# A hybrid decoder layer on one core: softmax of one block ahead of the other's masks, and longer stretches of one product width

## The chip, the cores and the metric

The kernel runs on one core of a Trainium2 chip. The metric is device time in microseconds, from the start to the end of one execution, as the median over several runs; lower is better. The engines are TensorE (PE in the profile; PEld is its weight loading), VectorE (DVE), ScalarE (ACT), GpSimd (POOL) and SyncE (SP, which issues the loads).

## What is computed

One decoder layer for a sequence of 256 positions, width 2048, in float32. Two mixers run side by side on the normalised input: an RG-LRU branch (a short convolution, a gated linear recurrence, times a GELU) and sliding-window attention with sinks (32 query heads, 4 key heads of 64, window 128, blocks of 128). They are merged by sigmoid gates and projected, and an MLP with squared ReLU follows. Cut from the reference:

```python
h = rmsnorm(x, norm_mix_pre)
xr, yr, q, k, v, g_rnn, g_attn = split(h @ w_in)
y_rnn = rg_lru(conv(xr)) * gelu(yr)
y_att = sliding_window_sink_attention(rope(q), rope(k), v, attn_sinks)
mix = sigmoid(g_rnn) * (y_rnn @ w_rnn_proj) + sigmoid(g_attn) * (y_att @ w_attn_proj)
x = x + rmsnorm(mix @ w_out, norm_mix_post)
u = square(relu(rmsnorm(x, norm_mlp_pre) @ w_mlp_up))        # 2048 -> 8192
x = x + rmsnorm(u @ w_mlp_down, norm_mlp_post)               # 8192 -> 2048
```

In attention the scores of 8 heads of a key head are masked, a maximum is taken over keys and sink, and `p / (sum p + exp(sink - m))` multiplies the values.

## The kernel before

**Split products.** Every large float32 product is made from parts: an operand is written as a high part and a low part, and TensorE adds high times high, high times low and low times high. Activations lie as pairs of parts. Weights come from memory in half-chunks of 512 KB (`wraw`, 128 x 1024): SyncE issues the loads, ScalarE casts the high part (`whi`, L94) and VectorE subtracts to get the low part (`wlo`, L95). The class `Stream` keeps this order for the whole kernel: `half()` hands out the next half-chunk, `ahead(j)` makes sure that the parts of six half-chunks (AHEAD = 6) beyond j have been asked for. There are six buffers each for `whi` and `wlo` and four for `wraw`, so a cast waits until TensorE has done with the half-chunk six places before.

**The three shapes of product.** `a_pair` (L243 to L261) makes 2 x 128 output channels for all 256 positions from 2048 inputs, out of four half-chunks, two per group of 128 channels (`f`). The high part of the weights multiplies the high and the low part of the activations at once, 512 columns wide (L253); the low part multiplies the high activations alone, 256 columns wide (L256). Each half-chunk holds eight tiles of 128 x 128, so it gives eight wide and eight narrow products. `a_pair` is called from `conv` and `gelu` (acts `hT`) and from the MLP's up pass (acts `h2T`); the first two pairs of the up pass are made by `up_step` and `up_pair` instead. At the end of a pair ScalarE copies the narrow half (L260) and VectorE adds the rest (L261). The gate and query passes (`b_pass512`, L271, L273, L275) use 512-wide products with three products per weight tile. The down pass (L1061) uses a seven-product scheme, all 512 wide.

**What sets the order.** The program is a Python trace of tiles; a scheduler gives each engine its instruction order by priority and dependence, and pins (`pin`) or `high_priority` fix some places. Side work is written as generators in the list `waiting`: `keys_values`, `attention(g, ...)`, the merge and `residual`. `pump()` advances the first of them by one `yield`, and the main passes call it once for each stage, so a `yield` is the unit of "one stage later" in the program text.

**Attention.** `attention(g)` rotates and transposes the queries, then `scores(tb, j, ...)` multiplies queries and keys of block `tb` into banks (L537), masks them (`s`, L543) and takes maxima (`stat`, L545). Block 0 sees one block of keys and needs one call, block 1 sees two and needs two. `softmax(tb)` combines maxima with the sink (L552 to L554), takes exponentials on ScalarE (L559, one per head), sums and inverts (L561, L562), and scales on VectorE (L564). `turn_probs(tb)` transposes the probabilities on TensorE (`pt`, L581) and copies the banks with ScalarE (L583); the products with the values (`po`, L607) follow.

**1/rms of the first norm.** `first_norm` runs in the first stage of `keys_values`: for each block of positions it writes 1/rms on a diagonal (`spread`, L424) and lets TensorE spread it over all partitions with a matrix of ones (`pr`, L425); ScalarE copies it to `rT` (L426), which `conv` and `gelu` read much later. The keys are rotated (`k`, L486) with sine and cosine tables (L463, `ss`, `cc`), transposed (`pk`, L503) and copied to `kT`.

**The MLP's start.** Products of the first up pairs for the first block of positions (`up_step(0, ...)`, L954, 256 wide) are put between the transposes of the second block's normalised input `h` (`ptr`, L898; `h` comes from VectorE, L892) in portions 26, 6, 6, 6.

Of the kernel before, what the change touches and what calls it, by code (L numbers as in the profile page):

```python
# [22 lines left out]
ALU = mybir.AluOpType  # L23
AX = mybir.AxisListType

P = 128
D = 2048
S = 256
TB = 2
# [137 lines left out]
def layer(tc, x, g_pre, pos_t, pos_row, inv_freq, vecs, sinks, gains, w_kv, w_q, w_xy, w_rg, w_g, w_rp, w_ap, w_out,  # L167
# [75 lines left out]
    def a_pair(acts, out, prio=0):  # L243


        ps = pair("ps")
        for f in range(2):
            both = ps[:, f].rearrange("p a b -> p (a b)")
            for half in range(2):
                hi, lo = ws.half()  # L250
                act = [acts[kt // 4][:, kt % 4] for kt in range(half * 8, half * 8 + 8)]
                for k, a in enumerate(act):
                    mm(both, hi[:, k * P : k * P + P], a.rearrange("p a b -> p (a b)"),  # L253
                       start=half == 0 and k == 0, stop=False)
                for k, a in enumerate(act):
                    mm(ps[:, f, 1, :], lo[:, k * P : k * P + P], a[:, 0, :], start=False,  # L256
                       stop=half == 1 and k == 7)
                pump()
        with tc.high_priority(prio) if prio else ExitStack():
            nc.scalar.copy(out, ps[:, :, 1, :])  # L260
            nc.vector.tensor_tensor(out, ps[:, :, 0, :], out, ALU.add)  # L261
# [145 lines left out]
    ws.ahead(ws.at - 1)  # L407
    r0, r0h = [], []
    rT = pa.tile([P, S], F32, name="rT")

    def first_norm():

        pr = bank(psm, "pr")
        spread = t2("spread")
        for tb in range(TB):
            r = rms(tb, 0)
            half = st[:, 16 + tb : 17 + tb]
            nc.vector.tensor_scalar(half, r, 0.5, None, ALU.mult)
            r0.append(r)
            r0h.append(half)  # L420
            for t in (cc, ss):
                nc.vector.tensor_scalar(t[:, tb], t[:, tb], r, None, ALU.mult)
            dg = spread[:, tb * P : tb * P + P]
            nc.vector.tensor_scalar(dg, ident, r, None, ALU.mult)  # L424
            mm(pr[:, tb * P : tb * P + P], ones, dg, start=True, stop=True)  # L425
        nc.scalar.copy(rT, pr[:, 0:S])  # L426

    pos_i = pa.tile([P, TB], I32, name="pos_i")
# [63 lines left out]
    def keys_values(banks):  # L492
        yield
        first_norm()
        for tb in range(TB):
            nc.scalar.activation(v_sb[:, tb, :], banks[tb][:, 256:512], AF.Copy, scale=r0[tb])
            k2 = t2("k2")
            k4 = k2.rearrange("p (g c d) -> p g c d", g=NKV, c=2)
            rope(banks[tb][:, 0:256], tb, NKV, [k4[:, :, 0, :], k4[:, :, 1, :]])
            yield  # L500
            ps = bank(psm, "pk")
            for g in range(NKV):
                nc.tensor.transpose(ps[:, g * P : g * P + P], k2[:, g * P : g * P + P], ident)  # L503
            nc.scalar.copy(kT[:, :, tb * P : tb * P + P], ps.rearrange("p (g t) -> p g t", g=NKV))
            yield

    yatt = []

    def attention(g, banks):
# [76 lines left out]

        last_group = g == NKV - 1
        scores(0, 0, [bank(psm, "sc") for par in range(2)])
        scores(1, 0, [bank(psb, "sc") for par in range(2)])
        if not last_group:  # L590
            scores(1, 1, two_banks("sc"))
        softmax(0)
        yield
        if last_group:
            scores(1, 1, [bank(psb, "sc") for par in range(2)])
        softmax(1)
        yield
        turn_probs(0)
        yield
# [355 lines left out]
                  start=(tb, kt) == (0, 0), stop=False)  # L955

    todo = [(j, k) for j in (0, 2, 1, 3, 4, 5) for k in range(8)]
    for q, n in enumerate((26, 6, 6, 6)):
        for j, k in todo[:n]:
            pin(up_step(0, j, k))  # L960
        del todo[:n]
# [323 lines left out]
```

## Time and profile before

| what | value |
|---|---|
| median of 3 runs | 1519.63 us (1518.05 to 1521.94) |
| the profiled execution | 1518.56 us |
| its span | 1516.8 us |
| mean granted TensorE clock | 0.997 |
| loads from memory | 288.60 MB read, 194 GB/s over the span |
| load of half a chunk (`wraw`) | 512.0 KB, 4.3 to 5.2 us to landing |

The span is the time between the first and the last instruction that the profile records; the execution's own time is 1.8 us longer, since it includes what lies around. In a row of groups the columns are line, engine, operation, out<-in, shapes, count, then busy time in us and mean ns of one, then the idle time just before such instructions and what ended it. In a waits row the last numbers are the total us, how often, and the longest. In the chain and the timeline the first two numbers are the start in us from the span's start, and the us that the piece takes; xN counts like instructions in a row, and a bracket tells the idle time ahead and who ended it. Matmuls overlap their neighbours, so the distance from start to start is the cost of one.

### The profile page before, as it was taken

The numbers are of one execution on the slowest core, as the hardware profiler recorded it, in microseconds if no ns is written. First come the engines' busy times: TensorE is split into PE (matmuls) and PEld (weight loads), VectorE is DVE, ScalarE is ACT, GpSimd is POOL, SyncE is SP. The second block draws the span as 40 slices with busy tenths as digits, with TensorE's granted clock in tenths as the row PEclk, the third lists the DMA queues.
The fourth block names the chain that finished last, engine by engine and source line by source line (L and its number), as shares of the span: only waits on it lengthen the run. The fifth ranks groups of instructions, "written<-read, shape, count | busy, mean of one in ns | idle before, by whom it ended". The sixth has DMA issues, their size and how long they took to land.

```text
span 1516.8 us, 20055 instructions
## 1 busy us (share of the span) xinstructions
PE 1496.4 (99%) x7600; PEld 1259.9 (83%) x7600; DVE 1103.0 (73%) x1377; ACT 828.7 (55%) x1143; POOL 5.5 (0%) x11
## 2 busy tenths in 40 slices
PE   9999999999999999999999999999999999999997
PEld 7787778788888888888888888888888888888885
DVE  6666677858769967555657866688886666688897
ACT  6554654747566756443355655555454555555453
POOL 0000000000000000000000000000000000000001
PEclk9999999999999999999999999999999999999998
DMA  6645445455646565555764755566667565566564
GB/s 253 219 143 187 142 131 182 150 186 165 218 157 221 168 208 194 192 183 193 270 220 138 271 192 189 183 189 215 218 200 239 198 189 187 181 236 207 208 212 176
DMA packets 82896, 296.20 MB, mean 195 GB/s; under 512 B 9712, under 2 KB 9968, under 8 KB 81648
## 3 DMA queue, kind: packets, MB, share of 16 engines
q1 hardware_dynamic: 79056, 284.43, 57.3%
q10 hardware_dynamic: 3744, 10.50, 1.9%
q8 instruction: 59, 0.97, 0.3%
q14 instruction: 37, 0.30, 0.1%
HBM read 288.60 MB, written 6.29 MB: 194 GB/s over the span
## 4 chain that ended last, share of the span: by engine, by line
PE 82%; DVE 9%; DMA 5%; ACT 2%; issue 2%; DVEq 0%; SPq 0%; ACTq 0%
PE ps L253 22%; PE ps L256 11%; PE dQ L1061 4%; DMA wraw<-in_w_dn 4%; PE pp L271 4%; PE pp L275 4%; PE pp L273 4%; PE g L271 3%; PE g L275 3%; PE g L273 3%; DVE wlo L95 3%; PE s L1061 2%; PE dP L1061 2%; PE q L273 2%; PE q L275 2%; PE q L271 2%
## 5 line engine op out<-in xcount | busy, mean ns | idle before, releaser
L95 DVE TENSOR_TENSOR wlo<-wraw,whi 128x1024 fp32r<-128x1024 f32 x523 | 635.1, 1223 | 314.0 <-ACT whi L94 313.1
L94 ACT CAST whi<-wraw 128x1024 fp32r<-128x1024 f32 x523 | 544.5, 1052 | 576.6 <-PE ps L253 134.2
L253 PE MATMUL ps<-h2T,whi 128*128 128x512 f32 x960 | 240.5, 393 | 0.0
L253 PEld LDWEIGHTS ps<-h2T,whi 128*128 128x128 f32 x960 | 172.8, 189 | 30.8
L256 PEld LDWEIGHTS ps<-h2T,wlo 128*128 128x128 f32 x960 | 131.0, 191 | 9.3
L256 PE MATMUL ps<-h2T,wlo 128*128 128x256 f32 x960 | 133.9, 283 | 0.0
L253 PE MATMUL ps<-hT,whi 128*128 128x512 f32 x512 | 129.7, 394 | 0.0
L1061 PE MATMUL dQ<-whi,uT 128*128 128x512 f32 x288 | 106.9, 389 | 0.0
L253 PEld LDWEIGHTS ps<-hT,whi 128*128 128x128 f32 x512 | 91.9, 189 | 17.6 <-issue 1.5
L271 PE MATMUL g<-whi,hT 128*128 128x512 f32 x256 | 101.3, 396 | 0.0
L273 PE MATMUL g<-wlo,hT 128*128 128x512 f32 x256 | 100.1, 391 | 0.1
L275 PE MATMUL g<-whi,hT 128*128 128x512 f32 x256 | 99.9, 390 | 0.0
L256 PEld LDWEIGHTS ps<-hT,wlo 128*128 128x128 f32 x512 | 69.9, 190 | 5.0
L256 PE MATMUL ps<-hT,wlo 128*128 128x256 f32 x512 | 71.6, 283 | 0.0
L1061 PEld LDWEIGHTS dQ<-whi,uT 128*128 128x128 f32 x288 | 54.1, 188 | 11.2
L271 PEld LDWEIGHTS g<-whi,hT 128*128 128x128 f32 x256 | 48.1, 188 | 10.5 <-issue 1.0
L1061 PE MATMUL dQ<-wlo,uT 128*128 128x512 f32 x144 | 56.2, 390 | 0.5 <-DVE wlo L95 0.5
L275 PEld LDWEIGHTS g<-whi,hT 128*128 128x128 f32 x256 | 48.1, 188 | 10.1
L273 PEld LDWEIGHTS g<-wlo,hT 128*128 128x128 f32 x256 | 48.2, 188 | 10.0 <-DVE wlo L95 0.5
L1061 PE MATMUL dCs<-whi,uT 128*128 128x512 f32 x144 | 54.1, 389 | 0.0
L1061 PE MATMUL dP<-whi,uT 128*128 128x512 f32 x144 | 54.1, 389 | 0.0
L130 DVE TENSOR_TENSOR tlo<-t,thi 128x1536 fp32r<-128x1536 f32 x28 | 49.2, 1757 | 5.4 <-ACT thi L129 5.3
(280 smaller groups left out, 2464.8 us busy)
## 6 DMA issues: line engine op xcount, KB each, us to landing
wraw<-in_w_up SPq DMA_DIRECT2D x128, 512.0 KB, 4.8
wraw<-in_w_dn SPq DMA_DIRECT2D x128, 512.0 KB, 4.6
wraw<-in_w_g SPq DMA_DIRECT2D x64, 512.0 KB, 4.5
wraw<-in_w_xy SPq DMA_DIRECT2D x64, 512.0 KB, 4.6
wraw<-in_w_q SPq DMA_DIRECT2D x32, 512.0 KB, 4.5
wraw<-in_w_ap SPq DMA_DIRECT2D x32, 512.0 KB, 4.4
wraw<-in_w_rp SPq DMA_DIRECT2D x32, 512.0 KB, 4.3
wraw<-in_w_out SPq DMA_DIRECT2D x32, 512.0 KB, 5.2
```

The lines of the kernel that those rows point to most:

```text
L94: self.pin(self.nc.scalar.copy(hi, src))
L95: self.pin(self.nc.vector.tensor_tensor(lo, src, hi.bitcast(F32), ALU.subtract))
L130: v.tensor_tensor(lo, t, hi.bitcast(F32), ALU.subtract)
L253: mm(both, hi[:, k * P : k * P + P], a.rearrange("p a b -> p (a b)"), start=half == 0 and k == 0, stop=False)
L256: mm(ps[:, f, 1, :], lo[:, k * P : k * P + P], a[:, 0, :], start=False, stop=half == 1 and k == 7)
L271: mm(banks[tb][n], a[:, 0, t], hi[:, n * 512 : n * 512 + 512], start=first, stop=False)
L273: mm(banks[tb][n], a[:, 0, t], lo[:, n * 512 : n * 512 + 512], start=False, stop=False)
L275: mm(banks[tb][n], a[:, 1, t], hi[:, n * 512 : n * 512 + 512], start=False, stop=last)
L1061: mm(b, a[x], w[y], start=not begun and i == 0, stop=tail and i == 2)
```

## The change

Four places change.

`a_pair` keeps its products but makes them in another order: with the half-chunks 0 to 3 of the pair, the high parts of 0 and 1 and the first product of 2 (17 wide products), then the low parts of 0, 1, 2 and 3 (32 narrow ones), then the rest of 2 and all of 3 (15 wide ones). The weights are asked for by `ws.ahead` a little later than before, at the places that the diff shows; `pump` is called four times as before.

In `attention`, `softmax(0)` is called before the scores of block 1 are masked, and two stages are added before `turn_probs(0)`.

The products that spread 1/rms leave `first_norm` for a function `spread_out`, called after the transposes of the first block's keys.

The first portion of `up_step` grows from 26 to 30 products.

```diff
--- before.py
+++ after.py
@@ -244,18 +244,41 @@
 
 
         ps = pair("ps")
-        for f in range(2):
-            both = ps[:, f].rearrange("p a b -> p (a b)")
-            for half in range(2):
-                hi, lo = ws.half()
-                act = [acts[kt // 4][:, kt % 4] for kt in range(half * 8, half * 8 + 8)]
-                for k, a in enumerate(act):
-                    mm(both, hi[:, k * P : k * P + P], a.rearrange("p a b -> p (a b)"),
-                       start=half == 0 and k == 0, stop=False)
-                for k, a in enumerate(act):
-                    mm(ps[:, f, 1, :], lo[:, k * P : k * P + P], a[:, 0, :], start=False,
-                       stop=half == 1 and k == 7)
-                pump()
+
+        def run(j, part, ks=range(8)):
+            f, half = j // 2, j % 2
+            for k in ks:
+                kt = half * 8 + k
+                a, w = acts[kt // 4][:, kt % 4], parts[j][part][:, k * P : k * P + P]
+                if part:
+                    mm(ps[:, f, 1, :], w, a[:, 0, :], start=False, stop=j == 1 and k == 7)
+                else:
+                    mm(ps[:, f].rearrange("p a b -> p (a b)"), w, a.rearrange("p a b -> p (a b)"), start=kt == 0,
+                       stop=j == 3 and k == 7)
+
+
+
+        at = ws.at
+        parts = [ws.half()]
+        run(0, 0)
+        parts.append(ws.half(False))
+        run(1, 0)
+        pump()
+        parts.append(ws.half(False))
+        run(2, 0, (0,))
+        run(0, 1)
+        ws.ahead(at + 1)
+        pump()
+        run(1, 1)
+        ws.ahead(at + 2)
+        run(2, 1)
+        parts.append(ws.half(False))
+        run(3, 1)
+        pump()
+        run(2, 0, range(1, 8))
+        ws.ahead(at + 3)
+        run(3, 0)
+        pump()
         with tc.high_priority(prio) if prio else ExitStack():
             nc.scalar.copy(out, ps[:, :, 1, :])
             nc.vector.tensor_tensor(out, ps[:, :, 0, :], out, ALU.add)
@@ -407,11 +430,10 @@
     ws.ahead(ws.at - 1)
     r0, r0h = [], []
     rT = pa.tile([P, S], F32, name="rT")
+    spread = t2("spread")
 
     def first_norm():
 
-        pr = bank(psm, "pr")
-        spread = t2("spread")
         for tb in range(TB):
             r = rms(tb, 0)
             half = st[:, 16 + tb : 17 + tb]
@@ -420,9 +442,12 @@
             r0h.append(half)
             for t in (cc, ss):
                 nc.vector.tensor_scalar(t[:, tb], t[:, tb], r, None, ALU.mult)
-            dg = spread[:, tb * P : tb * P + P]
-            nc.vector.tensor_scalar(dg, ident, r, None, ALU.mult)
-            mm(pr[:, tb * P : tb * P + P], ones, dg, start=True, stop=True)
+            nc.vector.tensor_scalar(spread[:, tb * P : tb * P + P], ident, r, None, ALU.mult)
+
+    def spread_out():
+        pr = bank(psm, "pr")
+        for tb in range(TB):
+            mm(pr[:, tb * P : tb * P + P], ones, spread[:, tb * P : tb * P + P], start=True, stop=True)
         nc.scalar.copy(rT, pr[:, 0:S])
 
     pos_i = pa.tile([P, TB], I32, name="pos_i")
@@ -502,6 +527,8 @@
             for g in range(NKV):
                 nc.tensor.transpose(ps[:, g * P : g * P + P], k2[:, g * P : g * P + P], ident)
             nc.scalar.copy(kT[:, :, tb * P : tb * P + P], ps.rearrange("p (g t) -> p g t", g=NKV))
+            if tb == 0:
+                spread_out()
             yield
 
     yatt = []
@@ -586,14 +613,16 @@
 
         last_group = g == NKV - 1
         scores(0, 0, [bank(psm, "sc") for par in range(2)])
+        softmax(0)
         scores(1, 0, [bank(psb, "sc") for par in range(2)])
         if not last_group:
             scores(1, 1, two_banks("sc"))
-        softmax(0)
         yield
         if last_group:
             scores(1, 1, [bank(psb, "sc") for par in range(2)])
         softmax(1)
+        yield
+        yield
         yield
         turn_probs(0)
         yield
@@ -955,7 +984,7 @@
                   start=(tb, kt) == (0, 0), stop=False)
 
     todo = [(j, k) for j in (0, 2, 1, 3, 4, 5) for k in range(8)]
-    for q, n in enumerate((26, 6, 6, 6)):
+    for q, n in enumerate((30, 6, 6, 6)):
         for j, k in todo[:n]:
             pin(up_step(0, j, k))
         del todo[:n]
```

How the order of instructions moves is shown at three places. Line numbers grow by 23 to 29 with the change: L543 becomes L570, L552 L579, L561 L588, L581 L608, L425 L450, L503 L528; in `a_pair` wide products are L256 and narrow ones L254 after it.

VectorE, attention of group 1, from the second pair of masks on; before (`mask_422` and `mask_423` are the same mask of both kernels):

```order
L543 SCALAR_TENSOR_TENSOR s<-sc,mask_422 128x512 x2
L545 TENSOR_REDUCE stat<-s 128x2 x2
L543 SCALAR_TENSOR_TENSOR s<-sc,mask_422 128x512 x2
L545 TENSOR_REDUCE stat<-s 128x2 x2
L552 TENSOR_TENSOR stat<-stat,sink 128x8
L95 TENSOR_TENSOR wlo_1437<-wraw_1277,whi_1436 128x1024
L553 TENSOR_SCALAR stat<-stat 128x8
L552 TENSOR_TENSOR stat<-stat,sink 128x8
L554 TENSOR_TENSOR stat<-sink,stat 128x8
L553 TENSOR_SCALAR stat<-stat 128x8
L554 TENSOR_TENSOR stat<-sink,stat 128x8
L95 TENSOR_TENSOR wlo_1467<-wraw_1308,whi_1466 128x1024
```

and with the change:

```order
L570 SCALAR_TENSOR_TENSOR s<-sc,mask_423 128x512
L579 TENSOR_TENSOR stat<-stat,sink 128x8
L570 SCALAR_TENSOR_TENSOR s<-sc,mask_423 128x512
L580 TENSOR_SCALAR stat<-stat 128x8
L572 TENSOR_REDUCE stat<-s 128x2
L581 TENSOR_TENSOR stat<-sink,stat 128x8
L572 TENSOR_REDUCE stat<-s 128x2
L570 SCALAR_TENSOR_TENSOR s<-sc,mask_423 128x512 x2
L572 TENSOR_REDUCE stat<-s 128x2 x2
L588 TENSOR_TENSOR stat<-stat 128x8
L579 TENSOR_TENSOR stat<-stat,sink 128x8
L589 RECIPROCAL stat<-stat 128x8
```

Block 0's statistics (the first L552, L553, L554) stood behind all masks and a low part of weights; now they stand among the first masks of block 1, and the low parts come after them.

TensorE, one `a_pair` of the up pass, its first two half-chunks before:

```order
L253 MATMUL ps<-h2T_6249,whi_8257 128x512 x4
L253 MATMUL ps<-h2T_6250,whi_8257 128x512 x4
L256 MATMUL ps<-h2T_6249,wlo_8258 128x256 x4
L256 MATMUL ps<-h2T_6250,wlo_8258 128x256 x4
L253 MATMUL ps<-h2T_6251,whi_8279 128x512 x4
L253 MATMUL ps<-h2T_6252,whi_8279 128x512 x4
L256 MATMUL ps<-h2T_6251,wlo_8280 128x256 x4
L256 MATMUL ps<-h2T_6252,wlo_8280 128x256 x4
```

and a stretch of one with the change, from the last wide product before the narrow ones:

```order
L256 MATMUL ps<-h2T_6249,whi_8369 128x512
L254 MATMUL ps<-h2T_6249,wlo_8310 128x256 x4
L254 MATMUL ps<-h2T_6250,wlo_8310 128x256 x4
L254 MATMUL ps<-h2T_6251,wlo_8339 128x256 x4
L254 MATMUL ps<-h2T_6252,wlo_8339 128x256 x4
L254 MATMUL ps<-h2T_6249,wlo_8370 128x256 x4
L254 MATMUL ps<-h2T_6250,wlo_8370 128x256 x4
L254 MATMUL ps<-h2T_6251,wlo_8384 128x256 x4
L254 MATMUL ps<-h2T_6252,wlo_8384 128x256 x4
L256 MATMUL ps<-h2T_6249,whi_8369 128x512 x3
```

Eight and eight alternate before; with the change the low parts of four half-chunks follow one another.

TensorE, first gate pass (`g`), where 1/rms is spread; before:

```order
L275 MATMUL g<-whi_399,hT_134 128x512
L425 MATMUL pr<-spread,ones 128x128
L271 MATMUL g<-whi_399,hT_134 128x512
L425 MATMUL pr<-spread,ones 128x128
L273 MATMUL g<-wlo_400,hT_134 128x512
L275 MATMUL g<-whi_399,hT_134 128x512
```

and with the change, some 38 gate products later, behind the first transposes of the keys:

```order
L296 MATMUL g<-wlo_480,hT_136 128x512
L298 MATMUL g<-whi_479,hT_136 128x512
L528 MATMUL pk<-ident,k_512 128x128 x4
L450 MATMUL pr<-spread,ones 128x128 x2
L294 MATMUL g<-whi_479,hT_136 128x512
L296 MATMUL g<-wlo_480,hT_136 128x512
```

The two products of `pr` stood one gate product apart ahead of the keys' transposes; now both stand behind them.

## The prediction

> **What bounds the kernel now.** I read the page first, then TensorE's waits, then the chain that ended last, then the timeline around each edit.
>
> ```profile
> span 1516.8 us, 20055 instructions
> PE 1496.4 (99%) x7600; PEld 1259.9 (83%) x7600; DVE 1103.0 (73%) x1377; ACT 828.7 (55%) x1143; POOL 5.5 (0%) x11
> PEclk9999999999999999999999999999999999999998
> L95 DVE TENSOR_TENSOR wlo<-wraw,whi 128x1024 fp32r<-128x1024 f32 x523 | 635.1, 1223 | 314.0 <-ACT whi L94 313.1
> L253 PE MATMUL ps<-h2T,whi 128*128 128x512 f32 x960 | 240.5, 393 | 0.0
> L253 PE MATMUL ps<-hT,whi 128*128 128x512 f32 x512 | 129.7, 394 | 0.0
> ```
>
> TensorE is busy for 99% of the span at a clock that never leaves the top digit. VectorE is at 73%, ScalarE at 55%, and the products of `a_pair` waited for nothing (0.0). So time can come only from two places: TensorE's stalls, and what its products cost in the stream. The waits view lists the stalls that were recorded:
>
> ```profile
> PE pt L581 <- DVE s L564: 3.6, 3, 1.4
> PE pr L425 <- DVE spread L424: 0.9, 1, 0.9
> PE ptr L898 <- DVE h L892: 0.7, 1, 0.7
> PE s L1061 <- DVE u L261: 0.6, 2, 0.3
> ```
>
> All the rows that the change aims at come to 5.8 us. For the price of a product I take the chain of waits, where start to start is the true spacing (the 393 ns of a row above is latency, with neighbours overlapping):
>
> ```profile
> 827.54 5.76 PE ps L998 x48
> 833.30 1.84 PE ps L995 x8
> ...
> 965.04 1.84 PE ps L253 x8
> ...
> 984.59 1.85 PE ps L253 x8
> ...
> 1067.77 2.72 PE dQ L1061 x12
> ```
>
> In a long stretch of one width a 512-wide product costs 2.72/12 = 226.7 ns and a 256-wide one 5.76/48 = 120.0 ns. Eight and eight would then take 1.813 + 0.960 = 2.773 us. In `a_pair`, from 965.04 to 984.59, seven periods of eight and eight take 19.55/7 = 2.793 us. **One alternation of width costs 20 ns** beyond its products. The eight wide ones behind the 48 narrow ones took 1.84 us, the same as behind eight narrow ones: a longer stretch does not make its edge dearer.
>
> **Part 1, longer stretches.** The same 64 products per pair now run as 32 wide, 32 narrow, since the 15 wide at a pair's end join the 17 at the start of the next: one alternation where there were four. The two counts above, (960 + 512)/32, give 46 pairs. 46 x 3 x 20 ns = 2.76; I take **2.7 us** (2.5 to 2.8; at the ends of the runs of pairs a part alternation stays). No instruction is added. What holds this up is that the low parts of four half-chunks must be there when the 32 narrow products start; see the third rival.
>
> The Trainium skill, "TensorE: Matmul & The Clock Gate", section "Back-to-back issue gap", gives the spacing of a warm product by its width alone, N/2.4 + 2.5 ns. By that the order of widths is worth nothing and this term would be 0. The trace disagrees on the size (216 and 109 ns by the rule, 226.7 and 120.0 measured) and shows the 20 ns that the rule has no room for.
>
> **Part 2, attention.** Groups 1, 2 and 3 stall at the first transposes of the probabilities. Group 1 and group 3:
>
> ```profile
> 160.91 0.39 PE L271 MATMUL q<-whi,hT 128*128 128x512 f32 x1
> 162.73 1.23 PE L581 MATMUL pt<-ident,s 128*128 128x128 f32 x8 [1.43 <-DVE s L564]
> ...
> 269.80 0.39 PE L253 MATMUL ps<-hT,whi 128*128 128x512 f32 x1
> 270.98 1.23 PE L581 MATMUL pt<-ident,s 128*128 128x128 f32 x8 [0.79 <-DVE s L564]
> 280.96 0.63 PE L581 MATMUL pt<-ident,s 128*128 128x128 f32 x4
> ```
>
> By starts, the product at 160.91 would be done after 0.23, at 161.14, so the loss is 1.59; in group 3 it is 0.95; group 2 shows the same 1.43 recorded. Together 4.1 us. Behind it stands softmax on VectorE and ScalarE:
>
> ```profile
> 149.36 1.28 DVE L543 SCALAR_TENSOR_TENSOR s<-sc,mask 128x512 f32<-128x512 f32 x2
> 150.56 1.27 DVE L545 TENSOR_REDUCE stat<-s 128x4 f32<-128x512 f32 x2
> ...
> 156.51 0.16 DVE L552 TENSOR_TENSOR stat<-stat,sink 128x8 f32<-128x8 f32 x1
> ...
> 161.89 1.29 DVE L564 TENSOR_TENSOR s<-s,stat 128x512 f32<-128x512 f32 x2
> ```
>
> ```profile
> 152.95 1.06 ACT L94 CAST whi<-wraw 128x1024 fp32r<-128x1024 f32 x1 [4.76 <-PE g L275]
> ...
> 158.24 0.39 ACT L559 ACTIVATE s<-s,stat 128x128 f32<-128x128 f32 x1
> ...
> 161.42 0.49 ACT L559 ACTIVATE s<-s,stat 128x256 f32<-128x256 f32 x1
> ...
> 279.06 0.49 ACT L559 ACTIVATE s<-s,stat 128x256 f32<-128x256 f32 x1
> ```
>
> Before, all masks and maxima (149.36 to 156.51) and a weight's low part come ahead of block 0's exponentials at 158.24. Now block 0's statistics stand behind its own four passes and, as the order shows, two masks and two maxima of block 1: 149.36 + 2.4 + four more passes of 0.6 gives about 154.1. The eight exponentials, 0.39 apart (158.24 to 161.42), end near 157.2, and sum, reciprocal and the scaling of 1.29 end near 159, or 159.6 with block 1's last masks between. TensorE arrives at about 160.6. The wait goes with about 1 us to spare.
>
> The change says "two stages later", but the order shows the first transposes directly behind the 48 gate products: one q product earlier than before in groups 1 and 2, seven in group 0, so 0.2 and 1.6 us earlier. In group 0, where the waits view names none, I count about 2 us to spare after that. The second block's transposes do move 48 products back in groups 0 to 2. What is late next: ScalarE's copies of the transposed banks and two low parts now stand behind the softmax. The cast at 152.95 had waited 4.76 us for TensorE to free a buffer, so six half-chunks stood ready, each good for 12 products of 0.227, 2.72 us; a slip of 5 us is covered, and uncovered costs up to 1.2 us per low part. I allow 0.1 for each of three groups at a bank copy. In group 3 block 1's exponentials cannot move up, since ScalarE ends them at 279.06 + 0.49 = 279.55 behind the same casts and copies, while TensorE is 0.8 earlier; the transposes at 280.96, with no wait before, then lose about 0.5 (0 to 0.9). Net 4.1 - 0.3 - 0.5 = **3.3 us** (1.8 to 4.4).
>
> **Part 3, 1/rms spread.**
>
> ```profile
> 45.10 0.49 PE L425 MATMUL pr<-spread,ones 128*128 128x128 f32 x2 [0.92 <-DVE spread L424]
> ...
> 49.04 1.28 ACT L463 ACT_TABLE_LOAD   x1
> ...
> 54.22 0.29 DVE L486 TENSOR_TENSOR k<-ra,rb 128x128 f32<-128x128 f32 x1
> 54.57 0.66 PE L503 MATMUL pk<-ident,k 128*128 128x128 f32 x4
> ```
>
> The 0.92 at 45.10 goes. But the keys' transposes at 54.57 come directly behind keys that VectorE ends at 54.22 + 0.29 = 54.51. Their chain runs from the table load at 49.04 through the sines and the rotation, not through TensorE. It comes forward only by the copy of the spread (about 0.4) that leaves ScalarE ahead of the load. TensorE would be there 1.6 us sooner (0.92, some 0.2 of start-up, and 0.5 for the two products now behind). So most of the wait reappears at the keys. Net **0.4 us** (-0.2 to 1.1).
>
> **Parts 4 and 5, MLP edges.**
>
> ```profile
> 812.90 3.27 PE L954 MATMUL ps<-h2T,whi 128*128 128x256 f32 x26
> 816.91 0.66 PE L898 MATMUL ptr<-ident,h 128*128 128x128 f32 x4 [0.74 <-DVE h L892]
> ...
> 999.48 0.50 PE L1061 MATMUL s<-thi,seven 128*128 128x512 f32 x1 [0.29 <-DVE u L261]
> ```
>
> Thirty instead of 26 products fill the 0.74 ahead of the second block's transposes with 4 x 0.12 = **0.5 us** (0.3 to 0.7) of work taken from after them. At the start of each of the two down passes, TensorE waits for the last pair's `u`; in the new order ScalarE's copy of that pair stands one weight cast (1.05 us) earlier, against 0.6 recorded in both. I take **0.4 us** (0 to 0.9).
>
> **Sum**: 2.7 + 3.3 + 0.4 + 0.5 + 0.4 = 7.3 us. The profiled execution took 1518.56 us, its span 1516.8; so 1509.5 for the span and 1511.3 for the execution. The median of the runs shown, 1519.63 (1518.05 to 1521.94), lies 1.1 above that execution, which gives **1512.3 us**. With the terms between their bounds together: 1509.6 to 1515.
>
> **Rivals.**
>
> First, the 20 ns are not the width's: they belong to the handover from one half-chunk to the next, which stays. For it: each period of eight and eight has exactly one handover. Against it: the 12 products in 2.72 at 1067.77 are one half-chunk each and pay no such edge, nor do the 48 narrow ones, which run over several. Then 7.3 - 2.7 = 4.6, **1515.0 us**. The formula of the Trainium skill cited above leads to the same.
>
> Second, the attention's gain is handed on. With both blocks' exponentials in one row on ScalarE, the casts behind them are late and TensorE waits for weights in the gate and q passes instead. For it: VectorE's low parts move behind the softmax and its page row shows 313 us spent waiting for casts. Against it: the six half-chunks ahead. Then 7.3 - 3.3 = 4.0, **1515.6 us**.
>
> Third, slower. The 32 narrow products use four low parts, one per 8 x 0.12 = 0.96 us, while VectorE makes one per 1.22 (1223 ns in its row). If the low parts are not made in advance, each stretch is short by at least 0.26, 46 x 0.26 = 12.0 us, and 12.0 - 7.3 = +4.7 gives **1524.3 us**; with all four made in the burst it would be up to three times that. Parts used in one stretch also free their buffers in one go, which favours bursts. It decides once the split's lead falls from six parts to under four, about 4 us late. Against it:
>
> ```profile
> 913.84 1.05 ACT L94 CAST whi<-wraw 128x1024 fp32r<-128x1024 f32 x1 [1.74 <-PE ps L253]
> ```
>
> In the midst of the MLP pairs ScalarE's cast waits for TensorE to give back a buffer, so the split is full and not behind; four low parts, 4.9 us, fit twice into a pair of 11.2 us, and by the buffers that come free a part is started some 10 us before its use.
>
> **How the numbers follow.** Forecast 0.72, first rival 0.08, second 0.11, third 0.09. About 0.3%, 4.6 us (to 1515.1), is what a measurement of this kernel can tell from no change. The first rival lies on that bound, half to each side; the second falls to no change; of the forecast's own cases a few hundredths fall short of it. So faster 0.74, same 0.16, slower 0.10. The forecast's own range is 1509.6 to 1515; to leave out no more than 2 in 10 I reach to 1508.9 below (all bounds kind) and, past the second rival, to 1517.0 above. The third is left out.
>
> **What would show it.** A period of 32 and 32 in `a_pair` takes 7.25 + 3.84 + 0.02 = 11.11 us instead of 4 x 2.793 = 11.17. In TensorE's waits the row of `pt` for `s` falls from 3.6 to under 0.8, `pr` for `spread` vanishes and a wait of 0.5 to 1.0 for `k` appears, `ptr` for `h` falls to about 0.3. The forecast is wrong if `a_pair`'s narrow products wait for `wlo`, if rows of `g` or `q` waiting for `whi` or `wlo` pass 1 us together, or if the period stays at 11.17.

## The result, and the profile after

| kernel | median | ratio to before, 95% interval |
|---|---|---|
| before, 20 runs | 1518.15 us | |
| changed, 20 runs | 1516.3 us (1512.98 to 1519.6) | 0.9987 (0.998 to 0.9994) |

Ratios are of fast executions; one execution of the experiment sixteens, at a mean clock of 0.654, took 2132.6 us and is not in its ratio. The change gains 0.13%, some 2 us; 7.3 were forecast. The profiled execution's span is 1515.4 us against 1516.8. The first lines of the changed kernel's page, and TensorE's waits:

```profile
span 1515.4 us, 20015 instructions
PE 1493.5 (99%) x7600; PEld 1261.9 (83%) x7600; DVE 1101.4 (73%) x1377; ACT 830.5 (55%) x1143; POOL 5.5 (0%) x11
PEclk9999999999999999999999999999999999999999
```

```profile
PE pt L608 <- ACT pT L610: 4.6, 3, 2.3
PE pt L608 <- DVE s L591: 1.6, 1, 1.6
PE ptr L375 <- DMA x<-in_x: 1.2, 1, 1.2
PE warm L366 <- DVE ones L350: 1.1, 1, 1.1
PE pk L528 <- DVE k L511: 0.8, 1, 0.8
PE dQ L1090 <- DVE wlo L95: 0.8, 1, 0.8
PE kv L396 <- DVE wlo L111: 0.4, 1, 0.4
PE ptr L927 <- DVE h L921: 0.3, 1, 0.3
```

The waits of `pt` for `s` fell from 3.6 to 1.6 us (under 0.8 was forecast), and a row is new: `pt` waits 4.6 us for `pT`, the copies of the transposed banks on ScalarE. To see what each edit brought, the span is cut at TensorE instructions that all kernels of this study share. The numbers are differences between starts in the profiled executions, in us:

| stretch on TensorE | before | changed | changed, again | pairs_only | no_attention | keys_later |
|---|---|---|---|---|---|---|
| start to first gate product (`g`) | 34.79 | 34.72 | 35.60 | 34.63 | 34.65 | 35.89 |
| to first scores (`sc`) | 58.52 | 58.30 | 58.34 | 58.42 | 61.18 | 57.24 |
| to first gate product of the recurrence (`pg`) | 252.08 | 254.66 | 253.07 | 252.01 | 251.97 | 251.97 |
| to the merge's transposes | 271.40 | 270.68 | 270.73 | 270.80 | 270.80 | 270.80 |
| to the last transpose of `h` | 204.25 | 204.22 | 204.25 | 204.25 | 204.25 | 204.25 |
| to the down pass (the first `dQ` from `thi`) | 177.32 | 176.00 | 176.01 | 176.49 | 176.01 | 176.00 |
| to the end | 518.42 | 516.81 | 516.40 | 516.87 | 514.96 | 517.04 |

The third row is attention, and it is the one that got longer: by 2.6 us in one execution of the changed kernel and 1.0 in another. All other stretches together got shorter by 4.0 in the first (1.4 + 2.6). In the first row, 35.60 and 35.89 go with a slow clock and not with an edit: the granted clock was 0.50 from 9.04 to 12.46 us in the one and from 9.38 to 12.79 in the other, and 1.00 there in the rest.

**What happens in attention.** ScalarE, then TensorE, in group 0 of the changed kernel (timeline; a bracket is idle time ahead and who ended it):

```profile
107.01 0.50 ACT L586 ACTIVATE s<-s,stat 128x256 f32<-128x256 f32 x1
...
107.50 2.93 ACT L94 CAST whi<-wraw 128x1024 fp32r<-128x1024 f32 x3
110.33 1.06 ACT L610 COPY s<-pt 128x512 f32<-128x512 f32 x2
...
115.73 1.05 ACT L94 CAST whi<-wraw 128x1024 fp32r<-128x1024 f32 x1 [2.24 <-DMA wraw<-in_w_q]
118.55 1.05 ACT L94 CAST whi<-wraw 128x1024 fp32r<-128x1024 f32 x1 [1.77 <-DMA wraw<-in_w_q]
119.83 1.05 ACT L94 CAST whi<-wraw 128x1024 fp32r<-128x1024 f32 x1 [0.24 <-DMA wraw<-in_w_g]
121.10 1.04 ACT L94 CAST whi<-wraw 128x1024 fp32r<-128x1024 f32 x1 [0.23 <-DMA wraw<-in_w_g]
122.06 1.06 ACT L610 COPY pT<-pt 128x512 f32<-128x512 f32 x2
```

```profile
118.68 1.03 PE L608 MATMUL pt<-ident,s 128*128 128x128 f32 x8
122.69 0.66 PE L608 MATMUL pt<-ident,s 128*128 128x128 f32 x4 [2.27 <-ACT pT L610]
```

Block 1's first eight transposes fill both banks of the pool by 119.7. The casts from 115.73 to 121.10 stand ahead of the copies in ScalarE's order, and each of them first waits for its weights to land (2.24, 1.77, 0.24 and 0.23 us). The copies do not overtake them: ScalarE stands idle for the last 0.23 us while both banks are full. The copies start at 122.06, and TensorE, which needs a bank for the next four transposes, stands still for 2.27 us. In the kernel before, the same copies came at 114.86, ahead of those casts:

```profile
111.64 1.04 ACT L583 COPY s<-pt 128x512 f32<-128x512 f32 x2
...
114.86 1.08 ACT L583 COPY pT<-pt 128x512 f32<-128x512 f32 x2
```

Why are the weights late? The row of DMA activity from 95 to 130 us in 40 slices (tenths of the engines' time; 0.875 us each), before and then changed:

```profile
DMA  4368200000039886100000002685778878476566
```

```profile
DMA  3377100000000000000049879997973898678400
```

Before, loads run in three bursts; changed, one long pause lies from 101 to 112.5 us. A `wraw` buffer is free once VectorE has subtracted the low part. SyncE's waits from 90 to 125 us show it (the last number is the longest wait), before and then changed:

```profile
SPq L76 <- DVE wlo L95: 23.1, 8, 9.6
```

```profile
SPq L76 <- DVE wlo L95: 30.1, 10, 15.9
```

Low parts that stood ahead of the scaling of block 0's probabilities now stand behind that of both blocks, and until they are made there is no buffer to load into. VectorE before (the second of two low parts there), then changed:

```profile
104.56 1.22 DVE L95 TENSOR_TENSOR wlo<-wraw,whi 128x1024 fp32r<-128x1024 f32 x1
```

```profile
108.06 2.50 DVE L591 TENSOR_TENSOR s<-s,stat 128x512 f32<-128x512 f32 x4
110.48 4.62 DVE L95 TENSOR_TENSOR wlo<-wraw,whi 128x1024 fp32r<-128x1024 f32 x4
```

A low part also needs its cast. ScalarE's casts stand behind the exponentials of both blocks now: before, one starts at 101.94 us, ahead of them; changed, none starts between 93.12 and 107.50. So both engines share in the pause.

```profile
101.94 1.05 ACT L94 CAST whi<-wraw 128x1024 fp32r<-128x1024 f32 x1 [1.66 <-PE g L275]
```

**The stall costs more than its length.** Windows of the changed kernel: length, busy us and count of PE, PEld, DVE, ACT, POOL, then the granted clock, the DMA share, GB/s:

```profile
122.50:127.00 4.50, 4.31 (x16) 3.65 (x17) 0.91 (x1) 1.79 (x4) 0.00 (x0) 0.62 0.82 258
124.00:126.70 2.70, 2.70 (x9) 2.22 (x8) 0.00 (x0) 0.59 (x1) 0.00 (x0) 0.50 0.79 232
```

After 2.27 us of standing still TensorE runs at half clock until 126.7, which loses about 4.5 x (1 - 0.62) = 1.7 us more. In the page's row of 40 slices this does not show.

**The pairs** look as forecast. The chain of the changed kernel, in the up pass:

```profile
966.53 3.83 PE ps L254 x32
970.36 7.28 PE ps L256 x32
977.64 3.83 PE ps L254 x32
```

64 products take 977.64 - 966.53 = 11.11 us, 0.06 less than 4 x 2.793.

### The profile page after: what moved, and what is told of

The parts are those of the page before. It is cut to its first block, busy times and chain, and to the rows that moved or that the text cites. A ratio compares the mean times of both kernels' runs of the same rounds, so it can differ in the third digit from the quotient of the medians.

```text
span 1515.4 us, 20015 instructions
## 1 busy us (share of the span) xinstructions
PE 1493.5 (99%) x7600; PEld 1261.9 (83%) x7600; DVE 1101.4 (73%) x1377; ACT 830.5 (55%) x1143; POOL 5.5 (0%) x11
## 4 chain that ended last, share of the span: by engine, by line
PE 77%; DVE 11%; DMA 6%; ACT 3%; issue 2%; DVEq 0%; SPq 0%; ACTq 0%
PE ps L256 21%; PE ps L254 11%; PE dQ L1090 4%; DMA wraw<-in_w_dn 4%; PE pp L296 4%; PE pp L298 4%; PE pp L294 4%; DVE wlo L95 4%; PE g L298 3%; PE g L294 3%; PE g L296 3%; PE s L1090 3%; PE dP L1090 2%; PE o L298 2%; PE o L296 2%
## 5 line engine op out<-in xcount | busy, mean ns | idle before, releaser
L256 PE MATMUL ps<-h2T,whi 128*128 128x512 f32 x960 | 223.9, 390 | 0.0
L256 PEld LDWEIGHTS ps<-h2T,whi 128*128 128x128 f32 x960 | 178.2, 188 | 35.6
L256 PE MATMUL ps<-hT,whi 128*128 128x512 f32 x512 | 121.2, 391 | 0.0
L254 PEld LDWEIGHTS ps<-h2T,wlo 128*128 128x128 f32 x960 | 119.1, 192 | 2.3
L254 PE MATMUL ps<-h2T,wlo 128*128 128x256 f32 x960 | 119.9, 283 | 0.0
L256 PEld LDWEIGHTS ps<-hT,whi 128*128 128x128 f32 x512 | 94.7, 188 | 20.1 <-issue 1.5
L254 PEld LDWEIGHTS ps<-hT,wlo 128*128 128x128 f32 x512 | 63.7, 192 | 1.2
L254 PE MATMUL ps<-hT,wlo 128*128 128x256 f32 x512 | 64.7, 283 | 0.0
```

The source lines that it names most:

```text
L254: mm(ps[:, f, 1, :], w, a[:, 0, :], start=False, stop=j == 1 and k == 7)
L256: mm(ps[:, f].rearrange("p a b -> p (a b)"), w, a.rearrange("p a b -> p (a b)"), start=kt == 0, stop=j == 3 and k == 7)
```

## The experiments

Each ratio is to the kernel before, on the same chip. "Stretch" is attention's, from the first scores to the first `pg`, in the profiled execution.

**1. pairs_only**: the kernel before with `a_pair` of the changed one.

```diff
-            for half in range(2):
-                hi, lo = ws.half()
...
+        run(0, 0)
...
+        run(1, 0)
...
+        run(2, 0, (0,))
+        run(0, 1)
...
+        run(1, 1)
...
+        run(2, 1)
...
+        run(3, 1)
...
+        run(2, 0, range(1, 8))
...
+        run(3, 0)
```

> The kernel before with the new order of products in a_pair alone. Theory: the long stretches are worth what the changed kernel's trace suggests, about 3.3 us in a_pair, and the last pair's copy ahead of the down passes another 1 us: some 4 us below the kernel before (ratio 0.9972), a period of 64 products near 11.1 us, narrow products that wait for no low part. Rival: the price belongs to the handover of half-chunks and the gain in the changed kernel came from elsewhere: ratio 1.000, period 11.17 us. Second rival: the low parts are short in the stretch of 32: slower, with waits of narrow products for wlo.

Measured: 0.9975 (0.9966 to 0.9984), 1515.09 us, a pair of 11.12 us, no wait of a narrow product for `wlo`. By the medians this part alone is worth more than the whole change; the intervals just overlap. The two waits at the start of the down passes (0.6 us in the row of waits, 0.9 by starts) are gone too.

**2. sixteens**: the kernel before with stretches of 16.

```diff
-            for half in range(2):
-                hi, lo = ws.half()
+            two = [ws.half() for half in range(2)]
+            for part in range(2):
+                for half in range(2):
+                    for k in range(8):
+                        kt = half * 8 + k
+                        a, w = acts[kt // 4][:, kt % 4], two[half][part][:, k * P : k * P + P]
...
```

> The kernel before with a_pair in stretches of 16 wide and 16 narrow products: two alternations of width per pair instead of four, while the handovers of half-chunks stay as they are. Theory (each alternation has a price): two thirds of what one alternation per pair saves, 46 x 2 x 20 to 24 ns = 1.8 to 2.2 us in a_pair, a pair of 11.13 us, ratio 0.9985. Rival (the handover has the price, or the longest stretch alone): 11.17 us a pair, ratio 1.000.

Measured: 0.9975 (0.9965 to 0.9986). The chain of this kernel:

```profile
961.00 3.65 PE ps L258 x16
964.66 1.91 PE ps L256 x16
966.57 3.65 PE ps L258 x16
970.23 1.91 PE ps L256 x16
972.14 3.65 PE ps L258 x16
```

64 products take 11.14 us, where four alternations take 11.17 and one takes 11.11: the price goes with the number of alternations, some 20 ns each, and the handovers, which stayed, have none. By the ratio this kernel gained more than its alternations, 46 x 0.03 = 1.4 us, as pairs_only did, and here too the waits at the start of the down passes are gone. The traces show why: ahead of the first down pass ScalarE's copy of the last pair starts 0.95 us after the pair's products, here and in pairs_only, and 1.9 us after them in the kernel before, where a weight cast stands between.

**3. no_attention**: the changed kernel with attention as before.

```diff
-        softmax(0)
         scores(1, 0, [bank(psb, "sc") for par in range(2)])
...
+        softmax(0)
         yield
...
         softmax(1)
         yield
-        yield
-        yield
         turn_probs(0)
```

> The changed kernel with attention as before. Theory: the attention edit costs about 3.5 to 4 us net, so this is 5 us below the kernel before (ratio 0.9967), with the waits of pt for s of the kernel before (3.6 us) and none of pt for pT. Rival: the attention edit gained what was forecast and another edit gave it back: then this is slower than the changed kernel, ratio about 1.001.

Measured: 0.9975 (0.9962 to 0.9987), 1514.61 us; waits of `pt` for `s` 4.4, none for `pT`; stretch 251.97. So by the stretch the attention edit costs 2.7 us in the first profile of the changed kernel and 1.1 in the second; the intervals of the times overlap. The profiled execution shows another stall, at the keys, and with it why the gain can fall short of 0.9967:

```profile
55.07 0.66 PE L528 MATMUL pk<-ident,k 128*128 128x128 f32 x4 [2.19 <-DVE k L511]
...
56.00:59.00 3.00, 3.00 (x10) 2.39 (x9) 1.62 (x5) 0.97 (x3) 0.00 (x0) 0.54 0.68 231
```

In this execution a load landed late (a cast waited 1.30 us for it), the keys came 1.3 us later, the wait was 2.19 us, and the clock halved for 3 us again (0.54 in the window behind it).

**4. early_no_yields and yields_only**: the two halves of the attention edit, each alone, with all other edits of the changed kernel.

```diff
         softmax(1)
         yield
-        yield
-        yield
         turn_probs(0)
```

> The changed kernel without the two added stages; softmax(0) stays ahead of block 1's masks. In the order the first transposes then stand behind 26 to 31 of the 48 gate products. Theory: the stages hold these transposes back, and without them TensorE reaches them 6 to 7 us after the scores while s is ready some 9 us after them: waits of pt for s of 2 to 3 us in each of groups 0 to 2, ratio 1.000 to 1.002; the waits for pT vanish. Rival: the stages alone are what costs and the early softmax is all gain: waits at pt below 2 us in all, ratio 0.994 to 0.996.

```diff
-        softmax(0)
         scores(1, 0, [bank(psb, "sc") for par in range(2)])
...
+        softmax(0)
         yield
```

> The changed kernel with the two added stages, but softmax(0) behind block 1's masks as before. Theory: the copies of block 1's banks stand behind weight casts that wait for loads because the transposes come 48 products later, so pt waits for pT 4 to 5 us in groups 0 to 2 here too, and the first transposes wait 1.4 us for s in groups 1 and 2: 4 to 5 us above no_attention, ratio 0.999 to 1.000. Rival: it is the early softmax that starves the loads: then no wait for pT, and the time is that of no_attention, ratio 0.9967.

Measured: early_no_yields 1.0002 (0.9992 to 1.0012), stretch 255.92, `pt` waits for `s` 6.9 us in 4 places, the longest 1.9, none for `pT`. yields_only 0.9997 (0.9988 to 1.0006), stretch 255.64, `pt` waits for `s` 4.5 and for `pT` 3.2. Both theories held in kind; the waits were 1.4 to 1.9 rather than 2 to 3 us, and 3.2 rather than 4 to 5. Each half alone costs about what the pairs gain. With the early softmax alone the scheduler puts the first transposes 17 to 22 products ahead of their place in the changed kernel, before the data is there; the stages hold them back, but carry block 1's copies behind the casts. In groups 1 and 2 yields_only waits 1.31 and 1.67 us for a bank, the changed kernel 0.99 and 1.35, so there the stages alone make the wait. In group 0 yields_only waits only 0.35 us for a bank where the changed kernel waits 2.4, and its loads pause as in the kernel before: the long pause belongs to the early softmax.

**5. second_none**: the two stages between the transposes of block 0 and block 1 taken out.

```diff
         turn_probs(0)
-        yield
-        yield
         turn_probs(1)
```

> The changed kernel without the two stages between the transposes of block 0 and those of block 1; everything else stays. Block 1's transposes then come 3 to 6 products behind block 0's instead of 48, and ScalarE's copies of their banks stand ahead of the weight casts that wait for loads. Theory (the place of the copies in ScalarE's queue is what cost): the 4 to 5 us of pt for pT go, and with them the slow stretch of TensorE in group 0; pt waits for s some 1 to 1.5 us in groups 1 and 2 since block 1's softmax is just ending: about 3 to 4 us below the changed kernel, ratio 0.9955 to 0.9970. Rival (the early softmax itself keeps the copies late): waits for pT of 3 us or more stay, ratio 0.998 to 0.999.

Measured: 1.0001 (0.9991 to 1.001), stretch 255.71: the forecast was wrong by 0.3 to 0.5%. The waits for `pT` went, as the theory said:

```profile
PE pt L608 <- DVE s L591: 5.3, 3, 1.8
PE pt L608 <- ACT s L610: 1.6, 1, 1.6
```

But the softmax of block 1 ends later than assumed, so that `pt` waits 5.3 us for `s`, and in group 0 1.6 us for block 0's own copies, which stand behind three casts. Behind the wait in group 1, 1.84 us, the clock halved for 3.4 us, which is 1.7 us more. Neither 3 nor 48 products behind is right.

**6. mid24 and mid12**: the distance between the two, 24 and 12 products; both with the keys' transposes later (experiment 7).

```diff
         turn_probs(0)
         yield
-        yield
         turn_probs(1)
```

and in mid12 also

```diff
-        waiting.append(attention(g, b_pass512(hT, [bank(psb, f"q{tb}") for tb in range(TB)])))
+        waiting.append(attention(g, b_pass512(hT, [bank(psb, f"q{tb}") for tb in range(TB)], 1)))
```

> The changed kernel with the keys' transposes 6 products later (as in keys_later) and one stage instead of two between the transposes of block 0 and block 1, which then stand 24 products apart instead of 48. ScalarE has two or three weight casts ahead of the copies instead of four or five, and the last of them waits for a load. Theory: waits for pT remain, some 1 to 1.5 us in each of groups 0 to 2, less than in the changed kernel; the stretch from the first scores to the first gate product of the recurrence takes 251 to 253.5 us (254.7 in the changed kernel, 252.0 with attention as before); ratio 0.9965 to 0.998. Rival (the loads are late because of the early softmax, wherever the copies stand): as the changed kernel, 254 us or more.

> As mid24, and the query pass calls for side work after each half-chunk, so that the transposes of block 1 stand 12 products behind those of block 0: late enough for its softmax, and with the copies ahead of the casts that wait for loads. Theory: pt waits for neither s nor pT in groups 0 to 2 (under 1.5 us together); only group 3 keeps 1.8 us for s; the stretch takes 248 to 250 us, and the kernel is 2 to 4 us below keys_later, ratio 0.9945 to 0.9957, the fastest of all. Rival (the gain of the early softmax is always handed on): the waits come back elsewhere in the stretch, which stays at 252 us or more.

Measured: mid24 1.0007 (0.9998 to 1.0017), stretch 256.59, waits for `pT` 6.4 us, up to 2.3, and a window at clock 0.66 behind one of them. mid12 0.9976 (0.9967 to 0.9986), stretch 253.25, waits for `pT` 4.2, up to 1.6. Both forecasts were too good, and both rivals named the stretch rightly (254 us or more, 252 us or more). ScalarE in mid24 and then in mid12, group 1:

```profile
167.45 2.00 ACT L94 CAST whi<-wraw 128x1024 fp32r<-128x1024 f32 x2
171.75 1.04 ACT L94 CAST whi<-wraw 128x1024 fp32r<-128x1024 f32 x1 [2.31 <-DMA wraw<-in_w_q]
172.70 1.06 ACT L613 COPY pT<-pt 128x512 f32<-128x512 f32 x2
```

```profile
166.43 1.99 ACT L94 CAST whi<-wraw 128x1024 fp32r<-128x1024 f32 x2
168.31 1.07 ACT L613 COPY pT<-pt 128x512 f32<-128x512 f32 x2
```

In mid24 the last cast ahead waits 2.31 us for a load. In mid12 no load is waited for, and the two casts themselves, 1.99 us, still make TensorE wait 1.59 us (`pt` at 168.96). Both place the copies behind casts, and that is the cost; the loads decide how large it is.

**7. keys_later**: no_attention with four more stages ahead of the first keys' transposes, which move by 6 products.

```diff
             yield
+            if tb == 0:
+                for _ in range(4):
+                    yield
             ps = bank(psm, "pk")
```

> The changed kernel with attention as before, and with the first block's keys transposed 6 gate products later (four stages in the program). Theory: the wait of pk for k (0.8 us in the changed kernel, 2.2 us and a slow stretch of TensorE in the profiled run of no_attention) falls under 0.3 us, since 6 products are 1.4 us: 1 to 3 us below no_attention, ratio 0.9955 to 0.997. Rival: the wait only moves to the next transposes or to the scores: ratio 0.9975 as no_attention.

Measured: 0.9969 (0.9959 to 0.9978), 1514.18 us, the fastest kernel of the study. No wait for `k` is left here. From the start to the first scores it takes 93.13 us, against 93.02 in the changed kernel and 95.83 in no_attention: nothing is gained on the changed kernel there, whose wait was 0.8, and the 57.24 of the table begins behind a first gate product that came 1.2 us late. Nor do 6 products, 1.4 us, cover a late load: in mid24, which moves the keys likewise, a cast waited 1.60 us for its load and `pk` 0.95 us for `k`. Its interval lies below the changed kernel's (0.998 to 0.9994) and overlaps no_attention's, so the difference between the last two is shown by one trace of each and not by the times.

**8. no_spread_move**: the changed kernel with 1/rms spread as before.

```diff
-            if tb == 0:
-                spread_out()
...
+            mm(pr[:, tb * P : tb * P + P], ones, dg, start=True, stop=True)
```

> The changed kernel with 1/rms spread where it was. Theory: the move took away 0.9 us of pr for spread and put 0.8 to 2.2 us of pk for k in its place, now and then with a slow stretch of TensorE behind it: this is 0 to 1 us faster than the changed kernel, ratio 0.998 to 0.9987, with the wait for spread back and none for k. Rival (the forecast): the move gains 0.4 us net: ratio 0.999.

Measured: 1.0 (0.9991 to 1.001), above the changed kernel. From the first gate product to the scores it took 58.57 us, against 58.30 with the move; so the move is worth 0.2 to 0.3 us. The profile's stretch is 258.27, with 6.6 us of waits for `pT`, up to 2.7, and two halvings of the clock behind them, 1.7 us each. The forecast, 0 to 1 us faster, missed; the difference in time lies in attention, where nothing was edited.

**9. after_again**: the changed kernel once more, unchanged.

> The changed kernel itself once more, for the spread between executions. Theory: ScalarE's queue and the landing of loads decide the waits for pT anew in each execution, and where TensorE stands still for 2 us or more its clock may halve for some 3 us; so the stretch from the first scores to the first gate product of the recurrence differs by 1 to 3 us from the 254.7 of the first profile while the other stretches stay within 0.7 us, and the ratio is 0.998 to 1.000. Rival (the order alone decides): the stretch is 254.7 within 0.3 us.

Measured: 0.9994 (0.9984 to 1.0004); stretch 253.07, the others within 1 us of the first profile (start to the first gate product 0.9, more than the 0.7 that was expected, all others at most 0.4). The first wait for `pT` was 2.2 us here too, but the clock stayed at 1.00 behind it. So the cost of attention in the same program differs by 1.6 us between executions, and what follows from no_spread_move is no more than that. Taken with the first comparison, the change gains 0 to 0.2%.

## Why the prediction came out as it did

The range held the time (1516.3 in 1508.9 to 1517.0), but the main case did not: a gain clear of noise was given 0.74, and the gain is smaller than 0.3%. That the range held was luck. The forecast's own range, 1509.6 to 1515, missed; the upper end had been set past the second rival. And the kernel before, from whose 1519.63 us the sum started, had a median of 1518.15 over 20 runs: 0.9987 of 1519.63 would be 1517.7, outside. The lower end does not come out of the terms either, since all kind bounds together are 9.9 us, which gives 1509.7 and not 1508.9. A reading was off without effect: the page's row of the clock before the change ends on an 8, so it does leave the top digit in the last slice.

- **Part 1, the pairs: right.** 0.06 us per pair, 46 x 0.06 = 2.8 us against 2.7 forecast. An alternation costs some 20 ns (pairs_only, sixteens). The spacing by width alone (the Trainium skill, "TensorE: Matmul & The Clock Gate", "Back-to-back issue gap", where it is the formula of an isolated product) would have made 11.11, 11.14 and 11.17 us equal.
- **Part 2, attention: wrong, and the reason for the whole miss.** Forecast was a gain of 3.3 us; the stretch lost 2.6 in one execution and 1.0 in another. The first half held: block 0's probabilities are scaled in time and `pt` in group 1 waits for nothing at its first transposes. The step that failed is the sentence on what is late next: it saw that the copies and two low parts now stand behind the softmax, put "0.1 for each of three groups at a bank copy", and covered the rest with six half-chunks that stood ready. That cover was for TensorE's weights and they never ran out. It was no cover for ScalarE's queue: casts that wait for a load, and not only the work of casts, stood ahead of the copies. The prediction had even noted that the second block's transposes move 48 products back, and gave that no price. Excess by starts at that place was 2.4, 1.2 and 1.5 us in groups 0 to 2, and 1.7 for the halved clock. With 1.8 in group 3 the stretch loses 8.6 us where it lost 4.1 before. It grew by 2.6 and not by 4.5, so some 1.9 were gained in small spacings, which were not taken apart.
- **Group 3**: 0.5 (0 to 0.9) was forecast for its second transposes, 1.62 us were recorded; the gain at its first ones, which now wait for nothing, went straight into these.
- **Part 3, 1/rms: right in kind and small.** The wait reappeared at the keys (0.8 recorded), as said; the first gate product to the scores takes 58.30 and 58.34 us with the move, 58.52, 58.42 and 58.57 without (before, pairs_only, no_spread_move): 0.2 us for 0.4 forecast. What the prediction missed is that this wait grows to 2.2 us when a load is late, and then costs clock as well.
- **Parts 4 and 5**: the 30 products gave 0.5 (176.49 to 176.00 us between pairs_only and the kernels that have them), as forecast. The waits at the down passes vanished wholly: 0.9 by starts, the upper end of 0 to 0.9, and as forecast because ScalarE's copy comes ahead of a weight cast.
- **Rivals.** The second, attention's gain handed on, came nearest: 1515.6 us against 1516.3. Its mechanism was casts late because of the exponentials; that is right for group 0, but what waited was a bank to be copied and not a weight, and in groups 1 and 2 the two stages alone suffice (yields_only). The third, low parts short in the long stretch, did not occur in any kernel with the new pairs. The first was refuted by sixteens.

The sum in the sizes of the first profile, pairs 2.8, attention -2.6, start 0.3, products 0.5, down 0.9, makes 1.9 us against 1.4 of the spans, with 0.2 counted twice for the four pairs in attention's stretch; the last stretch alone varies by more than that between kernels (514.21 to 518.42 us).

## What to carry to other kernels

When work is moved later on TensorE, find what its results need on the other engines, and read what stands ahead of that in the queue there at the new time: an instruction that waits for a load blocks everything behind it, however little work it is. Deep buffers for one consumer are no cover for another that shares the producer's queue. And an order that a scheduler makes is only as good as its idea of when data is ready: two edits that repair each other in part (softmax early, transposes held back) each cost 3 us or more alone.

## What was not expected of the hardware

Behind some stalls TensorE's granted clock fell to 0.50. Apart from the first and the last 13 us of the spans, the kept traces show seven falls: one each in the changed kernel, no_attention, early_no_yields, second_none and mid24, two in no_spread_move. Each lasted 3.41 us and so cost about 1.7 us. Windows inside a fall, of early_no_yields, second_none and no_spread_move (twice):

```profile
160.00:162.00 2.00, 2.00 (x7) 1.61 (x6) 0.54 (x1) 2.00 (x9) 0.00 (x0) 0.50 0.20 45
```

```profile
167.00:169.50 2.50, 2.50 (x11) 2.31 (x12) 1.81 (x2) 2.30 (x4) 0.00 (x0) 0.50 0.63 198
```

```profile
123.30:126.70 3.40, 3.40 (x13) 2.93 (x13) 0.56 (x1) 1.45 (x3) 0.00 (x0) 0.50 0.77 236
181.30:184.70 3.40, 3.40 (x12) 2.82 (x11) 0.00 (x0) 1.09 (x2) 0.00 (x0) 0.50 0.81 266
```

The length of a stall does not sort the cases: the clock fell behind 1.84 us (second_none, group 1) and stayed at 1.00 behind 2.18 us (changed kernel, second execution) and 2.34 us (mid24, group 0). What sorts them is where the stall lies. In the traces' records of the clock, every change of one trace lies a whole number of 3.413 us after its first record; the two falls of no_spread_move begin at 123.28 and 181.31 us, and 58.03 us are 17 x 3.413. Cut into windows on that grid, the window just before each of the seven falls holds 1.84 to 2.72 us of idle TensorE. No other window holds more than 1.67, but for one of 1.86 without a fall. The 2.18 us lie on two windows, with 0.32 and 1.86, and the 2.34 us too, with 1.24 and 1.10. So about 1.85 us of idle time in one window is the bound in these runs. Since the grid starts elsewhere in each execution, the same stall of 2 us sometimes costs 1.7 us more and sometimes nothing. In the first 13 us this count does not sort the cases: the clock fell after windows with 1.62 to 1.73 us and not after one with 1.86.

The Trainium skill, "TensorE: Matmul & The Clock Gate", section "Part 1: The HAM clock gate", has the clock set by a free-running window of some 3.4 us. The traces agree, with 3.413 us. The section also names an idle window of about 3.4 us as the condition for the fall; here 1.84 us within one window were enough.
